# Gate and up of small experts in two matmul passes, with expert weight tiles split in one piece

## The chip, the core and the metric

One core of a Trainium2 chip runs the whole program once. The metric is the device time of that run in microseconds. The profile is one profiled execution of the same program; times inside it count from its first instruction.

## The reference, cut to what matters

A block with a token mixer and a mixture-of-experts layer is followed by a second block with attention, retention and a dense MLP. The change touches the expert layer, and how weight tiles are split in all layers. 512 tokens each go to 8 of 64 experts:

```python
N_EXPERTS, TOP_K, D_MODEL, D_EXPERT = 64, 8, 1024, 256

def swiglu(h, w_gu, w_down):
    gate, up = jnp.split(h @ w_gu, 2, axis=-1)
    return (jax.nn.silu(gate) * up) @ w_down

def expert_block(acc, blk):
    tok, wts, e = blk
    out = swiglu(h_pad[tok], w_gu[e], w_down[e])
    return acc.at[tok].add(out * wts[:, None]), None
```

Gate and up of one expert are a [tokens x 1024] by [1024 x 512] product, down is a [tokens x 256] by [256 x 1024] product. Everything is float32.

## The kernel before, in words

**Split numbers.** Every float32 operand of a large product is held as two tiles of the type float32r: `hi`, a copy that ScalarE (ACT) rounds, and `lo`, the rest, which VectorE (DVE) forms as the difference. `mm3` (lines 142 to 148) makes one product of three matmuls: x_hi by w_hi, x_hi by w_lo, x_lo by w_hi. In the expert layer the tokens are the stationary operand and the weights stream past as 512 columns.

**Weight units.** Weights come in units of 1 MB, 128 partitions of 2048 numbers. `load_unit` (line 113) issues one DMA on SyncE's queue (SP) into one of the `raw` buffers: three, and two more in the expert layer. `split_unit` (line 121) takes a unit in two halves of 1024 columns (`PIECES = 2`): each half has its own pair of tiles `whi`, `wlo`, its ACT copy (line 132) and its DVE difference (line 133). There are six such half tiles (two more in the expert layer, from `grow`, line 1130), given out in turn by `Turns`, and `Rows` (line 55) makes two halves look like one unit. A `raw` buffer is free when both differences are done, a half tile when TensorE (PE) is done with it.

**The expert layer.** `order` sorts the experts by their number of tokens, and `plan` (line 1149) gives each place in that order a capacity (`CAPS`): three of 192, six of 128, 21 of 96, 24 of 64 and 8 of 32, and ahead of them two experts of 128 whose place is fixed. It makes 44 groups: 12 pairs of 64 and 64 tokens, which share a block of 128 rows; 8 pairs of 96 and 32, also one block; 13 single experts of 96; 8 of 128; 3 of 192, in two blocks of 128 and 64. The groups are mixed evenly over the layer. That is 47 blocks, and three units of weights (two for gate and up, one for down) for each of 64 experts. An expert with more tokens than its capacity would be taken up by a loop behind a condition (lines 1312 to 1326).

For each group the rows of its blocks are gathered by an indirect DMA from GpSimd (POOL), turned on PE by `expert_rows` (line 985) into tiles `xT` hi and lo of 8 x 128 columns, and multiplied in `expert_in` (line 998): 8 steps of `mm3` an expert and block, into one PSUM tile `mm` of 512 columns. There the whole block is stationary, also in a pair: each expert of a pair computes all of the block's rows and only its own are read. ACT then takes the silu of the first 256 columns and DVE multiplies by the others (lines 1011 and 1012). `expert_turn` and `expert_out` (lines 1014 and 1025) do the down product of the group before, `expert_parts` and `expert_add` add 384 of the 1024 columns by matmuls into PSUM, and `expert_send` adds the other 640 in DRAM by an indirect DMA. All PSUM tiles of the layer but the sums are four banks of the tag `mm`.

The order on each engine is set by the tile framework's scheduler when the program is built; each engine then works strictly in that order.

Of the kernel before, what the change touches and what calls it, by code (L numbers as in the profile page):

```python
# [10 lines left out]
F = mybir.dt.float32  # L11
R = mybir.dt.float32r
# [9 lines left out]
T = 512  # L22
# [6 lines left out]
UNIT = 2048  # L29
PIECES = 2  # L30
PIECE = UNIT // PIECES
# [23 lines left out]
class Rows:  # L55


    def __init__(self, tiles, n, a):
        self.tiles, self.n, self.rows = tiles, n, a

    def __getitem__(self, at):
        p, k, *rest = at
        return self.tiles[k // self.n][(p, k % self.n, *rest)]


class Kernel:
    def __init__(self, ctx, tc, ins, out):
        self.tc, self.nc, self.ins, self.out = tc, tc.nc, ins, out
        self.ctx = ctx
        pool = lambda name, bufs=1, **k: ctx.enter_context(tc.tile_pool(name=name, bufs=bufs, **k))  # L70
        self.const = pool("const")
        self.raws = Turns((pool("wraw", RAW_BUFS, side="right"), RAW_BUFS))
        self.splits = Turns((pool("wsplit", SPLIT_BUFS * PIECES), SPLIT_BUFS * PIECES))
# [47 lines left out]
    def split_unit(self, parts, a, b, engine=None, rv=None):  # L121

        nc = self.nc
        if rv is None:
            rv = self.load_unit(parts if isinstance(parts, list) else [(None, parts)], a, b)
        n = min(a, a * PIECE // UNIT) if a * b == UNIT else a
        tiles = []
        for k in range(0, a, n):
            sp = self.splits.next()
            hi = sp.tile([128, PIECE], R, tag="hi", name="whi")[:, :n * b].rearrange("p (a b) -> p a b", a=n)  # L130
            lo = sp.tile([128, PIECE], R, tag="lo", name="wlo")[:, :n * b].rearrange("p (a b) -> p a b", a=n)
            nc.scalar.activation(hi, rv[:, k:k + n], AF.Copy)  # L132
            (engine or nc.vector).tensor_sub(lo, rv[:, k:k + n], hi.bitcast(F))  # L133
            tiles.append((hi, lo))
        hv, lv = (Rows([t[i] for t in tiles], n, a) for i in range(2))
# [4 lines left out]
        return hv, lv  # L140
# [21 lines left out]
    def fm_chunk(self, ps, w, x, j, n=T, x0=0):  # L162

        kk = w[0].rows
# [820 lines left out]
    def expert_rows(self, tiles, pp, xg, m=128):  # L985
# [3 lines left out]
        xT = [pool.tile([128, KD, 128], R, tag=tag, name="xT", bufs=2)[:, :, 0:m] for tag in tags]  # L989
        for u in range(2):  # L990
# [4 lines left out]
            self.split_ps(xT[0][:, 4 * u:4 * u + 4], xT[1][:, 4 * u:4 * u + 4], p2)  # L995
        return xT

    def expert_in(self, pp, gu, blocks, between=None):
# [3 lines left out]
        for u in range(2):  # L1002
            w = self.split_unit(gu[u].rearrange("p (k n) -> p k n", k=4), 4, 512)
            for ps, (xT, *_) in zip(pss, blocks):
                for k in range(4):
                    kk = 4 * u + k
                    self.mm3(ps[0:xT[0].shape[2]], [z[:, kk] for z in xT], [z[:, k] for z in w], kk == 0, kk == KD - 1)
            if u == 0 and between:
                between()
        for ps, (xT, a, p0, p1) in zip(pss, blocks):  # L1010
            nc.scalar.activation(a[p0:p1], ps[p0:p1, 0:256], AF.Silu)
            nc.vector.tensor_mul(a[p0:p1], a[p0:p1], ps[p0:p1, 256:512])  # L1012
# [30 lines left out]
    def expert_parts(self, mp, y, row, bufs=2):  # L1043
# [3 lines left out]
        yh, yl = (mp.tile([128, CA], R, tag=f"eys{i}", name="eys", bufs=bufs)[0:m] for i in range(2))  # L1047
        nc.scalar.activation(yh, y[0:m, :CA], AF.Copy)  # L1048
        last = nc.gpsimd.tensor_sub(yl, y[0:m, :CA], yh.bitcast(F))  # L1049
        oh = mp.tile([128, T], R, tag="eoh", name="eoh", bufs=bufs)[0:m]  # L1050
# [36 lines left out]
    def first_block(self):  # L1087
# [9 lines left out]
        with tc.tile_pool(name="route", bufs=1) as keep:  # L1097
# [7 lines left out]
            with ExitStack() as mctx, ExitStack() as ectx:  # L1105
# [24 lines left out]
                def grow():  # L1130
                    hctx.close()
                    sp = ectx.enter_context(tc.tile_pool(name="wsplit2", bufs=PIECES))
                    self.splits = Turns(*splits.pools, (sp, PIECES))
# [12 lines left out]
            self.raws, self.splits = raws, splits  # L1146
# [23 lines left out]
    def experts(self, mp, pp, h2d, cb, acc, shared, gT, sums, grow, ahead, extra):  # L1170
# [42 lines left out]
        def turn(g):  # L1213

            if g < len(groups):
                xT[g] = []
                for b in groups[g][1]:
                    free.append(xg_of[count[1]])
                    xT[g].append(self.expert_rows(tiles, pp, free[-1], b[-1][2]))
# [26 lines left out]
        tiles = more, ("xT0", "xT1")  # L1246
# [9 lines left out]
        for g in range(len(groups) + 1):  # L1256
# [36 lines left out]
            if g < len(groups):  # L1293
# [3 lines left out]
                for j, e in enumerate(es):  # L1297
                    e = number(e)
                    now[2].append(e)
                    self.expert_in(pp, gu(e), [(xT[g][b], a[b], p0, p1) for b, parts in enumerate(bs)  # L1300
                                               for i, p0, p1, _ in parts if i == j], None if j else advance)
# [9 lines left out]
        total = self.further(xp)  # L1311
        with tc.If(total > 0):
            cnt = xp.tile([128, 1], F, name="xcnt")
            nc.vector.memset(cnt, 0.0)
            with tc.For_i(0, total):
# [5 lines left out]
                self.expert_in(pp, gu(ev), [(self.expert_rows(tiles, pp, xgs[0]), a, 0, 128)])  # L1321
                y = mp.tile([128, D], F, tag="ey", name="ey", bufs=2)
                self.expert_out(pp, dn(ev), [(self.expert_turn(more, pp, a), wt, y, 0, 128)])
                self.expert_add(acc, *self.expert_parts(xp, y, row, 1)[0])
# [47 lines left out]
    def each_unit(self, ctx, w, loaded=(), engines=()):  # L1372

        sp = ctx.enter_context(self.tc.tile_pool(name="wsplit3", bufs=PIECES))
# [4 lines left out]
        turns = Turns((base, n - PIECES), (sp, PIECES), (base, PIECES))  # L1379
# [580 lines left out]
```

## Time and profile before

| | us |
|---|---|
| median of 3 runs (lowest, highest) | 2128.33 (2125.3, 2130.84) |
| the profiled execution's own time | 2128.15 |
| its span, first to last instruction | 2126.4 |
| PE busy | 2038.1 (96%) |
| DVE busy | 1425.5 (67%) |
| ACT busy | 1090.8 (51%) |
| POOL busy | 486.2 (23%) |

The span is shorter than the execution's time by 1.75 us. Shares of a whole span are means over stages with different limits, so the table only says that PE is nearly always at work; what a saved instruction is worth has to be read in its stage. In the rows below PE is TensorE's matmuls, PEld its loads of the stationary operand, SPq the queue of SyncE; "DMA share" is the mean busy share of the 16 DMA engines and PEclk the granted share of TensorE's 2.4 GHz.

### The profile page before, as it was taken

The numbers are of one execution on the slowest core, as the hardware profiler recorded it, in microseconds if no ns is written. First come the engines' busy times: TensorE is split into PE (matmuls) and PEld (weight loads), VectorE is DVE, ScalarE is ACT, GpSimd is POOL, SyncE is SP. The second block draws the span as 40 slices with busy tenths as digits, with TensorE's granted clock in tenths as the row PEclk, the third lists the DMA queues.
The fourth block names the chain that finished last, engine by engine and source line by source line (L and its number), as shares of the span: only waits on it lengthen the run. The fifth ranks groups of instructions, "written<-read, shape, count | busy, mean of one in ns | idle before, by whom it ended". The sixth has DMA issues, their size and how long they took to land. (4 is left out here: it accounts for less than half of the span.)

```text
span 2126.4 us, 28083 instructions
## 1 busy us (share of the span) xinstructions
PE 2038.1 (96%) x10311; PEld 1663.4 (78%) x10311; DVE 1425.5 (67%) x2444; ACT 1090.8 (51%) x1569; POOL 486.2 (23%) x307
## 2 busy tenths in 40 slices
PE   7999999999899999999999996999999999999998
PEld 4777888877787788877887784877788878888886
DVE  6667767647899799989999785455853345333344
ACT  7445443233387788878887884334232224232232
POOL 0322231011144343524334213011100001010110
PEclk9999999999899999999999998999999999999999
DMA  7211136633499899999999885312122333222221
GB/s 297 70 41 48 53 111 261 235 110 147 177 322 335 290 341 352 339 325 307 337 336 337 289 290 188 132 60 70 50 89 79 114 115 116 92 100 99 99 80 40
DMA packets 69713, 386.68 MB, mean 182 GB/s; under 512 B 11374, under 2 KB 12351, under 8 KB 30020
## 3 DMA queue, kind: packets, MB, share of 16 engines
q1 hardware_dynamic: 56932, 357.56, 45.6%
q0 software_dynamic: 12640, 27.29, 5.5%
q8 instruction: 82, 1.34, 0.2%
q14 instruction: 59, 0.48, 0.1%
HBM read 369.99 MB, written 23.55 MB: 185 GB/s over the span
## 5 line engine op out<-in xcount | busy, mean ns | idle before, releaser
L133 DVE TENSOR_TENSOR wlo<-raw,whi 128x1024 fp32r<-128x1024 f32 x586 | 728.0, 1258 | 252.0 <-ACT whi L132 244.0
L132 ACT ACTIVATE whi<-raw 128x1024 fp32r<-128x1024 f32 x592 | 621.0, 1057 | 385.6 <-PE mm L147 190.7
L146 PE MATMUL mm<-whi,xT 128*128 128x512 f32 (+2 forms) x536 | 219.7, 410 | 0.1
L147 PE MATMUL mm<-wlo,xT 128*128 128x512 f32 (+2 forms) x536 | 211.9, 395 | 0.0
L148 PE MATMUL mm<-whi,xT 128*128 128x512 f32 (+2 forms) x536 | 211.9, 395 | 0.0
L1039 POOL DMA_INDIRECT cb<-ey,sgi x67 | 130.9, 1954 | 233.4 <-ACT ey L1035 148.4
L146 PE MATMUL mm<-hT,whi 128*128 128x512 f32 x320 | 127.0, 397 | 0.0
L147 PE MATMUL mm<-hT,whi 128*128 128x512 f32 x320 | 125.8, 394 | 0.0
L148 PE MATMUL mm<-hT,wlo 128*128 128x512 f32 x320 | 125.5, 392 | 0.0
L147 PE MATMUL mm<-x,whi 128*128 128x512 f32 x304 | 122.5, 403 | 0.0
L148 PE MATMUL mm<-x,wlo 128*128 128x512 f32 x304 | 120.8, 398 | 0.0
L146 PE MATMUL mm<-x,whi 128*128 128x512 f32 x304 | 120.8, 397 | 0.0
L148 PEld LDWEIGHTS mm<-whi,xT 128*128 128x128 f32 (+2 forms) x536 | 96.8, 181 | 27.8
L146 PEld LDWEIGHTS mm<-whi,xT 128*128 128x128 f32 (+2 forms) x536 | 97.2, 181 | 23.1 <-DVE act L1012 0.5
L1565 POOL TENSOR_TENSOR relu<-relu 128x512 f32<-128x512 f32 x32 | 42.9, 1341 | 315.0 <-ACT relu L1563 315.0
L147 PEld LDWEIGHTS mm<-wlo,xT 128*128 128x128 f32 (+2 forms) x536 | 97.2, 181 | 22.3
L1049 POOL TENSOR_TENSOR eys<-ey,eys 128x384 fp32r<-128x384 f32 (+2 forms) x47 | 79.2, 1686 | 141.2 <-ACT eys L1048 114.3
L148 PE MATMUL mm<-whi,eaT 128*128 128x512 f32 (+2 forms) x268 | 105.8, 396 | 0.4 <-DVE eaT L153 0.2
L147 PE MATMUL mm<-wlo,eaT 128*128 128x512 f32 (+2 forms) x268 | 105.8, 395 | 0.0
L146 PE MATMUL mm<-whi,eaT 128*128 128x512 f32 (+2 forms) x268 | 105.8, 395 | 0.0
L146 PE MATMUL mm<-y,whi 128*128 128x512 f32 (+2 forms) x272 | 103.2, 380 | 0.0
L148 PE MATMUL mm<-y,wlo 128*128 128x512 f32 (+2 forms) x272 | 103.1, 379 | 0.0
(534 smaller groups left out, 4488.9 us busy)
## 6 DMA issues: line engine op xcount, KB each, us to landing
raw<-in_w_expert_gu SPq DMA_DIRECT2D x128, 1024.0 KB
raw<-in_w_expert_down SPq DMA_DIRECT2D x64, 1024.0 KB
raw<-in_w_in SPq DMA_DIRECT2D x41, 1024.0 KB
raw<-in_w_ff SPq DMA_DIRECT2D x32, 1024.0 KB
raw<-in_w_ada SPq DMA_DIRECT2D x24, 1024.0 KB
raw<-in_w_out SPq DMA_DIRECT2D x8, 1024.0 KB
raw<-in_w_v SPq DMA_DIRECT2D x4, 1024.0 KB
raw<-in_w_ret_up SPq DMA_DIRECT2D x4, 1024.0 KB
```

What stands on the lines that cost most here:

```text
L132: nc.scalar.activation(hi, rv[:, k:k + n], AF.Copy)
L133: (engine or nc.vector).tensor_sub(lo, rv[:, k:k + n], hi.bitcast(F))
L146: mm(ps, ah, bh, start=start, stop=False)
L147: mm(ps, ah, bl, start=False, stop=False)
L148: mm(ps, al, bh, start=False, stop=stop)
L1039: self.nc.gpsimd.indirect_dma_start(out=cb, out_offset=bass.IndirectOffsetOnAxis(ap=gi, axis=0), in_=y[p0:p1, CA:], in_offset=None, bounds ...
L1049: last = nc.gpsimd.tensor_sub(yl, y[0:m, :CA], yh.bitcast(F))
L1565: nc.gpsimd.tensor_mul(sq, r, r)
```

## The change

Four things, the first two of which the title names.

- `expert_in`: where a block's part holds up to 64 tokens (the pairs of 64, the 32 of a pair, the second block of a 192), hi and lo of those tokens stand side by side as one stationary operand of up to 128 columns. Two matmuls a step, by w_hi and by w_lo, give x_hi's product in the first rows of the PSUM tile and x_lo's in the rows behind; ACT copies the second lot to a tile `esum`, DVE adds the first, and silu and product follow from `esum`. The product x_lo by w_lo comes along. `expert_rows` lays the tiles out for it; the block of a 96 and a 32 takes four split instructions more.
- `split_unit`: one pair of tiles for the whole unit. In the expert layer (`cuts` is 1 there) one ACT copy and one DVE difference of 2048 columns do it; elsewhere it is still two and two, but the tile is free only as a whole. There are three whole tiles, and one more in the expert layer.
- The last sum (`add()`) stands ahead of the conditional loop instead of behind it.
- The conditional loop shares buffers with the layer.

```diff
 def split_unit(self, parts, a, b, engine=None, rv=None):
-        n = min(a, a * PIECE // UNIT) if a * b == UNIT else a
-        tiles = []
+        n = a // self.cuts if a * b == UNIT else a
+        sp = self.splits.next()
+        hi, lo = (sp.tile([128, UNIT], R, tag=t, name="w" + t)[:, :a * b].rearrange("p (a b) -> p a b", a=a)
+                  for t in ("hi", "lo"))
         for k in range(0, a, n):
-            sp = self.splits.next()
-            hi = sp.tile([128, PIECE], R, tag="hi", name="whi")[:, :n * b].rearrange("p (a b) -> p a b", a=n)
-            lo = sp.tile([128, PIECE], R, tag="lo", name="wlo")[:, :n * b].rearrange("p (a b) -> p a b", a=n)
-            nc.scalar.activation(hi, rv[:, k:k + n], AF.Copy)
-            (engine or nc.vector).tensor_sub(lo, rv[:, k:k + n], hi.bitcast(F))
+            nc.scalar.activation(hi[:, k:k + n], rv[:, k:k + n], AF.Copy)
+            (engine or nc.vector).tensor_sub(lo[:, k:k + n], rv[:, k:k + n], hi[:, k:k + n].bitcast(F))
...
 def expert_rows(self, tiles, pp, xg, parts=((0, 128),)):
+            x = pool.tile([128, KD, 256], R, tag=tags[0], name="xT", bufs=2)
+            if len(parts) == 1:
+                at = 128 if w > 64 else w
+                hi, lo = x[:, :, 0:w], x[:, :, at:at + w]
+                cut, out = [(lambda z: z, hi, lo)], [(hi, lo) if w > 64 else (x[:, :, 0:2 * w],)]
+            elif w == 64:
+                v = x.rearrange("p k (j h w) -> p k h j w", j=2, h=2)
+                cut = [(lambda z: z.rearrange("p k (j w) -> p k j w", j=2), v[:, :, 0], v[:, :, 1])]
+                out = [(x[:, :, 0:128],), (x[:, :, 128:256],)]
+            else:
+                cut = [(lambda z: z[:, :, 0:w], x[:, :, 0:w], x[:, :, 256 - w:256]),
+                       (lambda z: z[:, :, w:m], x[:, :, w:m], x[:, :, m:256 - w])]
+                out = [(x[:, :, 0:w], x[:, :, 256 - w:256]), (x[:, :, w:256 - w],)]
...
 def expert_in(self, mp, pp, gu, blocks, between=None):
-                    self.mm3(ps[0:xT[0].shape[2]], [z[:, kk] for z in xT], [z[:, k] for z in w], kk == 0, kk == KD - 1)
+                    if len(xT) == 2:
+                        self.mm3(ps[0:xT[0].shape[2]], [z[:, kk] for z in xT], [z[:, k] for z in w],
+                                 kk == 0, kk == KD - 1)
+                    else:
+                        for i, z in enumerate(w):
+                            nc.tensor.matmul(ps[0:xT[0].shape[2]], xT[0][:, kk], z[:, k],
+                                             start=kk == i == 0, stop=kk == KD - 1 and i == 1)
...
+                n = p1 - p0
+                s = mp.tile([128, 512], F, tag="esum", name="esum", bufs=2)[p0:p1]
+                nc.scalar.activation(s, ps[n:2 * n], AF.Copy)
+                nc.vector.tensor_add(s, ps[0:n], s)
+                nc.scalar.activation(a[p0:p1], s[:, 0:256], AF.Silu)
+                nc.vector.tensor_mul(a[p0:p1], a[p0:p1], s[:, 256:512])
...
+        add()
         with tc.If(total > 0):
...
-        add()
```

Counted over the whole built program, PE has 280 fewer matmuls of 512 columns (35 parts of up to 64 tokens, 8 each). ACT has 392 copies of 1024 columns fewer and 196 of 2048 more, DVE likewise; each has 35 instructions more for `esum`.

On PE, the end of gate and up of a pair of 64 and 64 tokens, its second unit and the start of the down product behind it; before (the numbers tell buffers apart):

```order
L146 MATMUL mm_6478<-whi_6515,xT_6243 128x512
L147 MATMUL mm_6478<-wlo_6516,xT_6243 128x512
L148 MATMUL mm_6478<-whi_6515,xT_6244 128x512
L146 MATMUL mm_6478<-whi_6515,xT_6243 128x512
L147 MATMUL mm_6478<-wlo_6516,xT_6243 128x512
L148 MATMUL mm_6478<-whi_6515,xT_6244 128x512
L146 MATMUL mm_6543<-whi_6535,eaT_6504 96x512
```

and in the changed program:

```order
L1018 MATMUL mm_6286<-whi_6311,xT_6066 128x512
L1018 MATMUL mm_6286<-wlo_6312,xT_6066 128x512
L1018 MATMUL mm_6286<-whi_6311,xT_6066 128x512
L1018 MATMUL mm_6286<-wlo_6312,xT_6066 128x512
L1041 MATMUL tp_6301<-ident_66,act_6084 128x96 x2
L131 MATMUL mm_6334<-whi_6330,eaT_6304 96x512
```

Each step has two matmuls instead of three, with one stationary tile instead of two, and a unit is one tile.

On DVE, at the same place of the layer; before, the product that frees the PSUM tile stands behind a difference of 1024 columns:

```order
L133 TENSOR_TENSOR wlo_6611<-raw_6608,whi_6610 128x1024
L153 TENSOR_TENSOR eaT_6505<-tp_6501,eaT_6504 128x2x96
L133 TENSOR_TENSOR wlo_6615<-raw_6608,whi_6614 128x1024
L133 TENSOR_TENSOR wlo_6667<-raw_6664,whi_6666 128x1024
L1012 TENSOR_TENSOR act_6468<-act_6468,mm_6478 64x256
L133 TENSOR_TENSOR wlo_6671<-raw_6664,whi_6670 128x1024
```

and in the changed program the addition of 512 columns that frees it comes behind one of 2048:

```order
L120 TENSOR_TENSOR wlo_6394<-raw_6391,whi_6393 128x2048
L138 TENSOR_TENSOR eaT_6305<-tp_6301,eaT_6304 128x2x96
L1031 TENSOR_TENSOR esum_6323<-mm_6286,esum_6323 64x512
L120 TENSOR_TENSOR wlo_6448<-raw_6445,whi_6447 128x2048
L1033 TENSOR_TENSOR act_6276<-act_6276,esum_6323 64x256
```

Of the 35 additions of the program, 10 stand directly behind two whole differences.

On ACT, again there, in the changed program:

```order
L137 ACTIVATE eaT_6304<-tp_6301 128x2x96
L1030 ACTIVATE esum_6323<-mm_6286 64x512
L1032 ACTIVATE act_6276<-esum_6323 64x256
L1056 ACTIVATE ey_6308<-mm_6334,swt_5194 96x512
L1069 ACTIVATE eys_6358<-ey_6308 96x384
```

Before, one silu stood there in place of the first two `esum` rows. The silu now waits for DVE's addition, and the copy `ey` that frees the next PSUM tile stands behind it; in 3 of the 35 cases the two follow each other directly like this, in the others at least one more instruction lies between.

## Rows read from the trace of the kernel before

**Rows 1.** Windows by stage: busy us of each engine (x instructions), PEclk, DMA share, GB/s.

```profile
600.00:1290.00 690.00, 685.20 (x3493) 545.95 (x3492) 613.24 (x889) 567.55 (x755) 270.54 (x153) 1.00 0.92 321
610.00:1290.00 680.00, 675.48 (x3430) 538.70 (x3429) 604.18 (x862) 559.35 (x744) 266.13 (x150) 1.00 0.92 322
...
1290.00:2126.40 836.40, 802.57 (x3681) 655.63 (x3679) 392.27 (x680) 268.43 (x412) 92.61 (x66) 0.98 0.27 93
```

**Rows 2.** Timeline of the expert layer, ten matmul starts apart: start us, us, engine, line.

```profile
816.02 0.39 PE L146 MATMUL mm<-whi,xT 128*128 128x512 f32 x1
...
818.35 0.40 PE L147 MATMUL mm<-wlo,eaT 128*128 128x512 f32 x1
```

**Rows 3.** Waits of PE, ACT and DVE, 610:1290: us in total, times, longest.

```profile
PE tp L908 <- DVE oh L903: 1.2, 3, 0.8
...
ACT whi L132 <- PE mm L148: 69.8, 134, 5.5
...
DVE wlo L133 <- ACT whi L132: 52.7, 81, 3.6
```

**Rows 4.** Waits of SyncE's DMA queue, 600:1290.

```profile
SPq L118 <- DVE wlo L133: 447.9, 156, 8.8
```

**Rows 5.** Groups by line and form, 610:1290: busy us, mean ns of one, idle before.

```profile
L133 DVE TENSOR_TENSOR wlo<-raw,whi 128x1024 fp32r<-128x1024 f32 x373 | 459.6, 1253 | 56.9 <-ACT whi L132 52.7
L132 ACT ACTIVATE whi<-raw 128x1024 fp32r<-128x1024 f32 x370 | 388.9, 1057 | 72.8 <-PE mm L148 69.8 <-DVE wlo L133 0.7 <-DVE srow L915 0.3
...
L153 DVE TENSOR_TENSOR xT<-tp,xT 128x512 fp32r<-128x512 f32 x56 | 35.9, 680 | 3.2 <-ACT xT L152 2.9
L152 ACT ACTIVATE xT<-tp 128x512 fp32r<-128x512 f32 x56 | 30.3, 594 | 6.1 <-PE mm L147 4.5 <-PE tp L994 1.2
...
L153 DVE TENSOR_TENSOR xT<-tp,xT 128x384 fp32r<-128x384 f32 x24 | 12.2, 550 | 1.0 <-ACT xT L152 0.7
...
L1012 DVE TENSOR_TENSOR act<-act,mm 64x256 f32<-64x256 f32 x27 | 11.2, 414 | 1.4 <-ACT act L1011 1.1
...
L152 ACT ACTIVATE xT<-tp 128x384 fp32r<-128x384 f32 x24 | 10.4, 487 | 0.2
L1011 ACT ACTIVATE act<-mm 64x256 f32<-64x256 f32 x27 | 10.2, 378 | 8.4 <-PE mm L148 8.4
...
L153 DVE TENSOR_TENSOR eaT<-tp,eaT 128x192 fp32r<-128x192 f32 x13 | 4.6, 351 | 0.9 <-ACT eaT L152 0.9
L152 ACT ACTIVATE eaT<-tp 128x192 fp32r<-128x192 f32 x13 | 4.1, 313 | 0.0
```

**Rows 6.** The tile wlo, 610:1290: DVE's differences, duration ns min/median/max.

```profile
L133 DVE TENSOR_TENSOR wlo<-raw,whi x373: 1204/1218/2776, 609.7 to 1280.8; 128x1024 fp32r<-128x1024 f32 x187
```

**Rows 7.** DMA of 610:1290: packets, and MB and share of 16 engines by queue.

```profile
DMA packets 38001, 218.85 MB, mean 322 GB/s; under 512 B 6867, under 2 KB 6867, under 8 KB 14265
...
q1 hardware_dynamic: 26641, 194.00, 75.6%
q0 software_dynamic: 11304, 24.16, 15.7%
```

**Rows 8.** Windows of 50 us: the densest of DVE and of the DMA engines in the layer.

```profile
600.00:650.00 50.00, 49.72 (x252) 40.12 (x251) 48.30 (x72) 43.56 (x58) 28.08 (x11) 1.00 0.93 343
...
1050.00:1100.00 50.00, 49.83 (x253) 40.15 (x252) 46.04 (x66) 43.61 (x58) 15.52 (x11) 1.00 0.98 363
```

**Rows 9.** Window of 10 us with the highest transfer rate of the layer.

```profile
920.00:930.00 10.00, 9.78 (x72) 8.10 (x71) 8.28 (x25) 6.48 (x9) 3.27 (x2) 1.00 1.00 405
```

**Rows 10.** Timeline at the layer's end: the sums of the last block, on PE.

```profile
1284.10 1.78 PE L1058 MATMUL acc<-eys,eoh 96*128 96x384 f32 x8
```

More of the change, by code (lines that the diff above doesn't have):

```diff
@@ L29 @@
 UNIT = 2048
-PIECES = 2
-PIECE = UNIT // PIECES
 VEC = {}
@@ L52, in next @@
         return order[(self.n - 1) % len(order)]
[L55 to L63, printed above, removed]
 class Kernel:
@@ L72, in __init__ @@
         self.raws = Turns((pool("wraw", RAW_BUFS, side="right"), RAW_BUFS))
-        self.splits = Turns((pool("wsplit", SPLIT_BUFS * PIECES), SPLIT_BUFS * PIECES))
+        self.splits = Turns((pool("wsplit", SPLIT_BUFS), SPLIT_BUFS))
+        self.cuts = 2
         self.dram = pool("scratch", space=DRAM)
@@ L139, in split_unit @@
             self.ticking = False
-        return hv, lv
+        return hi, lo
     def mm3(self, ps, a, b, start, stop):
@@ L162, in fm_chunk @@
     def fm_chunk(self, ps, w, x, j, n=T, x0=0):
-        kk = w[0].rows
+        kk = w[0].shape[1]
         for k in range(kk):
@@ L983, in gather, with expert_rows @@
                                           bounds_check=T - 1, oob_is_err=False)
-    def expert_rows(self, tiles, pp, xg, m=128):
+    def expert_rows(self, tiles, pp, xg, parts=((0, 128),)):
         nc = self.nc
         pool, tags = tiles
-        xT = [pool.tile([128, KD, 128], R, tag=tag, name="xT", bufs=2)[:, :, 0:m] for tag in tags]
+        m = parts[-1][1]
+        w = parts[0][1]
+        if len(tags) == 2:
+            hi, lo = (pool.tile([128, KD, 128], R, tag=tag, name="xT", bufs=2)[:, :, 0:m] for tag in tags)
+            cut, out = [(lambda z: z, hi, lo)], [(hi, lo)]
+        else:
[12 more added lines that the diff above has]
+                out = [(x[:, :, 0:w], x[:, :, 256 - w:256]), (x[:, :, w:256 - w],)]
         for u in range(2):
@@ L994, in expert_rows, with expert_in @@
                 nc.tensor.transpose(p2[:, k], xg[0:m, c:c + 128], self.ident[0:m, 0:m])
-            self.split_ps(xT[0][:, 4 * u:4 * u + 4], xT[1][:, 4 * u:4 * u + 4], p2)
-        return xT
-    def expert_in(self, pp, gu, blocks, between=None):
+            for some, hi, lo in cut:
+                self.split_ps(hi[:, 4 * u:4 * u + 4], lo[:, 4 * u:4 * u + 4], some(p2))
+        return out
+    def expert_in(self, mp, pp, gu, blocks, between=None):
         nc = self.nc
@@ L1218, in turn @@
                     free.append(xg_of[count[1]])
-                    xT[g].append(self.expert_rows(tiles, pp, free[-1], b[-1][2]))
+                    xT[g].append(self.expert_rows(tiles, pp, free[-1], [p[1:3] for p in b]))
                     rows_of.setdefault(g, []).append(count[1])
@@ L1245, in experts @@
         more = grow()
-        tiles = more, ("xT0", "xT1")
+        tiles = more, ("xT",)
         room(mp, AHEAD2)
@@ L1299, in experts @@
                     now[2].append(e)
-                    self.expert_in(pp, gu(e), [(xT[g][b], a[b], p0, p1) for b, parts in enumerate(bs)
-                                               for i, p0, p1, _ in parts if i == j], None if j else advance)
+                    self.expert_in(mp, pp, gu(e), [(xT[g][b][i], a[b], p0, p1) for b, parts in enumerate(bs)
+                                                   for i, (k, p0, p1, _) in enumerate(parts) if k == j],
+                                   None if j else advance)
                     finish()
```

30 lines of the change are left out of this document (16 added, 14 removed).

## The prediction

> **What bounds the kernel now.** I read the windows by stage first, because the change acts almost only in the expert layer, from 600 to 1290 us [rows 1]. In those 690 us TensorE is busy for 685.2, VectorE for 613.2, ScalarE for 567.6, and the 16 DMA engines have a mean share of 0.92. Four resources are close together; the reader is to see that TensorE is first, but with little distance to the next. The timeline says that TensorE's busy time is real: eleven matmuls start evenly between 816.02 and 818.35 [rows 2], 0.233 us apart, at the granted clock of 1.00, that is 2.4 GHz [rows 1]. The waits say the same from the other side [rows 3]: TensorE's longest wait for a tile is 1.2 us in all of 680, while ScalarE's copies wait 69.8 us for TensorE to give a split tile back and VectorE's differences 52.7 us for those copies. SyncE's loads wait 447.9 us for VectorE to free a raw buffer [rows 4]: data come as fast as they are used up. So TensorE sets the pace, and the work behind it runs ahead until its buffers are full.
>
> A rule that speaks against this reading: the Trainium skill, Perfetto Trace Analysis, section "Identifying the Most-Contended Engine", says that matmul busy time misleads and that the busy share of the weight loads is to be taken instead. Here that share is 546.0 of 690, 79% [rows 1]; by the rule TensorE would have a fifth of its time to spare, and matmuls taken away would give nothing: the time would stay at 2128 us. The even starts and the direction of the waits decide against it here, and I keep a small chance for it (the fourth case below).
>
> **The change part by part.** The sum is made against the profiled execution's own 2128.15 us, which is 0.2 below the median of 2128.33.
>
> *Matmuls removed.* 35 parts of up to 64 tokens lose 8 matmuls each: 280 x 0.233 = 65.2 us of TensorE [rows 2]. Fewer weight loads go with them. TensorE's stage would be 690 - 65 = 625 us if nothing else bound it.
>
> *Whole differences and copies.* The trace has no instruction of 2048 columns here. Above, it costs two halves, so nothing is saved; below, I go by how cost grows: VectorE from 680 ns at 512 columns [rows 5] to a median of 1218 at 1024 [rows 6], 538 per 512 columns, so 1218 + 1076 = 2294 ns, 142 less than two halves; ScalarE from 594 to 1057 [rows 5], so 1983 ns, 131 less. I take these, since rows of both engines grow by a fixed amount per column. For the layer's 187 units (373 halves [rows 5]) it is 26.6 us off VectorE and 24.5 off ScalarE.
>
> *Sums added.* 35 copies and 35 additions of 512 columns, the first of them out of PSUM. Nearest rows: 594 ns on ScalarE, 680 on VectorE [rows 5], hence 20.8 and 23.8 us. The silu and the product keep 378 and 414 ns [rows 5]; reading SBUF they could be a little cheaper or dearer, at most some tens of ns each, under 2 us. The 8 blocks of 96 and 32 split in two cuts, twice a block: on VectorE 550 + at most 351 instead of 680 [rows 5], 3.5 us more in all; on ScalarE 487 + 313 instead of 594, 3.3 us. Net, VectorE 613.2 - 26.6 + 23.8 + 3.5 = 613.9 us and ScalarE 567.6 - 24.5 + 20.8 + 3.3 = 567.2: both unchanged. What one part of the change saves on them the other spends.
>
> *Transfers.* None are added or taken away: 0.92 x 690 = 635 us of all 16 engines [rows 1].
>
> *What is late next.* Without TensorE's 65 us the highest floors are the DMA engines' 635, TensorE's 625 and VectorE's 614. None is reached at 100%: the densest 50 us of this layer show the DMA engines at 0.98 and VectorE at 48.3 of 50 [rows 8]. 635 / 0.98 = 648 us, and VectorE's 613.9 / 0.966 = 636. So I put the stage at 648, a gain of 42 of the 65; the wait that takes the place is ScalarE's for a raw tile that has not landed, and TensorE's behind it. The bounds: 690 - 625 = 65 if the DMA share is no floor; 690 - 661 = 29 if the DMA engines stay at 0.96.
>
> *Is the share a floor?* In the same section the skill wants the transfer rate, not the engines' occupancy, as the measure for DMA, and its section "Engine Utilization" gives 358 GB/s as a core's peak, about 435 at most for one core alone. By that, 321 GB/s is 90% or 74%, the floor is 619 us or lower, and the case below in which TensorE stays the bound would hold. The trace shows 405 GB/s over one stretch of 10 us [rows 9], so 358 is no limit here; but at shares of 0.98 the mean of 50 us is 363 GB/s [rows 8], because row gathers and scatters take 15.7% of the engines for 24 of 219 MB [rows 7]. I stay with the share.
>
> *Other stages.* Elsewhere a unit is still split in two cuts, but its tile comes free as a whole. Where that is late once, it costs a half's copy and difference, 1.06 + 1.22 = 2.3 us [rows 5, 6]; at two stage entries (the output projection, the second block) 4.6 us. The scheduler also moves some differences behind other work, which can as well gain. From 1290 us on TensorE is busy 802.6 of 836.4 us [rows 1] and covers the rest. I take 0, with ends of -5 and +5. The sums ahead of the condition are 8 matmuls of 1.78 us [rows 10] that TensorE does at the same place either way: 0, at most 1.8. If no loop pass runs, its buffers cost nothing.
>
> The sum: 2128.15 - 42 = **2086 us**, 2073 to 2099 with the DMA share between 1.00 and 0.96.
>
> **Rivals.** (1) *TensorE stays the bound.* The share of DMA is elastic, loads just overlap more, and VectorE fits. For it: 405 GB/s at 920 us [rows 9], and loads are never waited for now. Against: both next floors lie within 10 to 11 us of TensorE's 625. Time: 2128 - 65 = 2063.
>
> (2) *Every group keeps its own bound.* The four split tiles and five raw buffers may not carry a surplus from one group to the next. The plan has 20 x 72 + 21 x 36 + 3 x 72 = 2412 matmuls, 562 us; the other 128 of 690 are 2.7 us for each of 47 blocks, so a pair took 72 x 0.233 + 2.7 = 19.5 us. Now its VectorE work is 6 x 2.29 + (604.2 - 459.6) / 47 [rows 1, 5] + two sums, 18.6 us or 19.2 at the density above; its transfers are 6 units of 2.78 us (75.6% of 680 by 185 units of 194 MB) and 2.3 of queue 0 (15.7% of 680 by 47) [rows 7], 19.0 or 19.3. A pair gains 0.3 us, 20 pairs 6; the three experts of 192 gain 8 x 0.233 each, 5.6. Against it: nine units of buffers are three experts' weights, and single experts and pairs alternate. Time: 2116.
>
> (3) *The sum holds PSUM.* A bank was free after silu, half a difference and product, 0.38 + 1.22 + 0.41 = 2.0 us; now after copy, addition and what stands ahead of it on VectorE: 0.59 + 2.29 + 0.68 = 3.6 with one whole difference, 5.9 with two, as the built order has it for 10 of 35. There are four banks, and behind the silu, which waits for the addition, ScalarE has the copies that free the others. If TensorE had to wait out all of it, 25 x 1.6 + 10 x 3.9 = 79 us come back for 65 saved: 2128 + 14 = 2142, slower. It decides from 65 / 35 = 1.9 us a sum. Against it: the matmuls behind it go to the three other banks, so only what is left after those are used up is a wait.
>
> (4) *No change.* Something other than TensorE already set the pace, as in the rule above, or waits return all of it: 2128.
>
> That the change does not do what it says is not open: the built order has the 280 matmuls fewer.
>
> **How the numbers follow.** Chances: 0.56 for the forecast, 0.15 for (1), 0.14 for (2), 0.08 for (4), 0.07 for (3). A measurement of this kernel tells 0.3% (6.4 us) from no change. Faster by more are the forecast, (1) and (2), 0.85; the same 0.08; slower 0.07. The range of 8 in 10 takes in the forecast's 2073 to 2099, (1) with 2063 less a little for other stages, and (2) with 2116: 2061 to 2116; the other two stay outside.
>
> **What would show it.** Right: the stage from about 600 us ends near 1248; DMA share about 0.98 in it; matmuls still 0.233 us apart where they run, but TensorE with some 20 us of gaps; differences of about 2.3 us and copies of about 2.0; ScalarE's wait for TensorE nearly gone, waits for landings in its place. Wrong: TensorE without gaps (1); VectorE full while TensorE waits in every pair (2); long waits of matmuls for the copies out of PSUM or the additions (3); or time lost before 600 or after the layer, which I put at nothing.

## The result, and the profile after

The change makes the kernel slower: 2148.86 us median of 4 runs (2141.99 to 2151.66) against 2127.07 (2125.3 to 2130.84, 4 runs); ratio 1.0097, 95% interval 1.0072 to 1.0121. I had forecast 2086 with a range of 2061 to 2116. The profiled execution after took 2151.66 us, the slowest of the four. Its first matmul on gathered rows comes at 585.5 us (585.7 before) and from the layer's end to the second block's first relu it takes 480.1 us (481.4 before); all of the loss lies in the expert layer, whose sums are taken out of PSUM from 1321.8 us on, 24.8 us later than the 1297.0 of before.

The windows of the layer, from 600 us to its end, first of the kernel before and then of the change; the columns are those of [rows 1]:

```profile
600.00:1297.00 697.00, 692.01 (x3522) 551.25 (x3520) 613.24 (x889) 567.57 (x756) 270.64 (x153) 1.00 0.91 318
```

```profile
600.00:1322.00 722.00, 664.81 (x3252) 508.33 (x3250) 619.15 (x757) 558.35 (x625) 328.89 (x153) 0.96 0.89 310
```

Nothing is full any more. TensorE is idle for 57 us where it was idle for 5; its granted clock is 0.96 of full in the mean, some 0.04 x 722 = 29 us of matmul work; and the transfers' share is lower than before, 0.89. So 65 us of matmuls went and some 52 + 29 came back as gaps and as slower matmuls; the 9 us left in the busy time make up the measured 25 more. The 29 is an estimate from a rounded share, and what the 9 are made of is not shown.

Waits of TensorE and of GpSimd, 610 to 1290 us (us in total, times, longest), first in the kernel before, where the scatter `cb` and the difference `eys` have other line numbers, then in the change:

```profile
PE acc L1058 <- POOL eys L1049: 1.1, 2, 0.9
...
POOL cb L1039 <- DMA cb<-ey,sgi: 45.3, 13, 8.1
```

```profile
PE acc L1079 <- POOL eys L1070: 19.5, 9, 3.6
PE mm L131 <- ACT eaT L137: 8.4, 9, 2.2
PE tp L1041 <- DVE act L1033: 4.8, 6, 1.7
PE mm L1018 <- DVE wlo L120: 3.6, 5, 1.0
...
POOL cb L1060 <- DMA cb<-ey,sgi: 62.9, 14, 6.2
POOL eys L1070 <- ACT eys L1069: 60.0, 17, 6.8
```

TensorE's longest waits do not go back to weight units that have not landed, as I had said, but to `eys`, the difference that GpSimd forms ahead of the additions into `acc`. GpSimd's own wait until the scatter before has landed was there before the change too, 45.3 us; TensorE was idle for 5 us all the same. One of TensorE's waits, in the timelines of GpSimd, TensorE and VectorE (start us, us, instruction, idle before it):

```profile
857.84 8.29 POOL L1060 DMA_INDIRECT cb<-ey,sgi  x1 [4.89 <-DMA cb<-ey,sgi]
865.71 1.45 POOL L1070 TENSOR_TENSOR eys<-ey,eys 96x384 fp32r<-96x384 f32 x1
...
863.26 0.40 PE L131 MATMUL mm<-whi,xT 128*128 128x512 f32 x1
867.21 1.48 PE L1079 MATMUL acc<-eys,eoh 96*128 96x384 f32 x7 [3.55 <-POOL eys L1070]
...
869.47 0.63 PE L132 MATMUL mm<-wlo,xT 128*128 128x512 f32 x1
869.90 0.63 PE L133 MATMUL mm<-whi,xT 128*128 128x512 f32 x1
...
856.82 4.48 DVE L120 TENSOR_TENSOR wlo<-raw,whi 128x2048 fp32r<-128x2048 f32 x2
...
862.62 2.28 DVE L120 TENSOR_TENSOR wlo<-raw,whi 128x2048 fp32r<-128x2048 f32 x1
```

The scatter waits 4.89 us until the scatter before it has landed, then its own issue takes 8.29 us while VectorE works through whole differences; `eys` stands behind it, TensorE waits 3.55 us, and its next matmuls start 0.43 us apart in place of 0.23 [rows 2]: it runs at 1.2 GHz.

The groups of the new instructions, 610 to 1290 us (busy us, mean ns | idle before), against [rows 5]:

```profile
L120 DVE TENSOR_TENSOR wlo<-raw,whi 128x2048 fp32r<-128x2048 f32 x183 | 423.1, 2325 | 40.2 <-ACT whi L119 38.8
...
L119 ACT ACTIVATE whi<-raw 128x2048 fp32r<-128x2048 f32 x183 | 347.8, 1912 | 35.7 <-PE mm L1018 20.4 <-PE mm L133 12.5 <-DMA raw<-in_w_expert_down 1.1
...
L1031 DVE TENSOR_TENSOR esum<-mm,esum 64x512 f32<-64x512 f32 x27 | 18.4, 680 | 2.1 <-ACT esum L1030 1.4
...
L1030 ACT ACTIVATE esum<-mm 64x512 f32<-64x512 f32 x27 | 16.0, 594 | 14.0 <-PE mm L1018 13.5
```

All four have the price that I gave them, within 4%. One price that I had kept did rise: the product, which now reads `esum` (414 ns before [rows 5]).

```profile
L1033 DVE TENSOR_TENSOR act<-act,esum 64x256 f32<-64x256 f32 x27 | 13.6, 502 | 3.6 <-ACT act L1032 3.3
```

That is 88 ns for each of 35, 3 us of VectorE. The prices were not the error.

### The profile page after: what moved, and what is told of

Read it like the earlier page. It is cut to its first block, busy times and chain, and to the rows that moved or that the text cites. A ratio compares the mean times of both kernels' runs of the same rounds, so it can differ in the third digit from the quotient of the medians.

```text
span 2150.0 us, 26943 instructions
## 1 busy us (share of the span) xinstructions
PE 2011.1 (94%) x10031; PEld 1620.6 (75%) x10031; DVE 1434.5 (67%) x2302; ACT 1070.3 (50%) x1427; POOL 549.6 (26%) x307
## 5 line engine op out<-in xcount | busy, mean ns | idle before, releaser
L120 DVE TENSOR_TENSOR wlo<-raw,whi 128x1024 fp32r<-128x1024 f32 (+1 forms) x393 | 709.6, 1823 | 247.7 <-ACT whi L119 242.1
L119 ACT ACTIVATE whi<-raw 128x1024 fp32r<-128x1024 f32 (+1 forms) x399 | 577.8, 1468 | 370.7 <-PE mm L132 211.1
L1060 POOL DMA_INDIRECT cb<-ey,sgi x67 | 155.6, 2323 | 258.7 <-ACT ey L1056 134.0
L966 POOL DMA_INDIRECT xg<-h2d,sgi x47 | 101.2, 2152 | 78.4 <-DVE srow L900 33.5
L1018 PE MATMUL mm<-wlo,xT 128*128 128x512 f32 (+1 forms) x280 | 114.2, 408 | 3.6 <-DVE wlo L120 3.6
L1018 PE MATMUL mm<-whi,xT 128*128 128x512 f32 (+1 forms) x280 | 115.6, 413 | 0.1
L131 PE MATMUL mm<-whi,xT 128*96 128x512 f32 (+1 forms) x256 | 109.0, 426 | 3.1 <-ACT ey L1056 2.9
L1056 ACT ACTIVATE ey<-mm,swt 64x512 f32<-64x512 f32 (+3 forms) x134 | 90.0, 680 | 41.9 <-PE mm L133 23.8
L132 PE MATMUL mm<-wlo,xT 128*96 128x512 f32 (+1 forms) x256 | 105.2, 411 | 2.9 <-DVE wlo L120 2.9
L1079 PE MATMUL acc<-eys,eoh 128*128 128x384 f32 (+2 forms) x376 | 85.7, 356 | 22.7 <-POOL eys L1070 21.6
L133 PE MATMUL mm<-whi,xT 128*96 128x512 f32 (+1 forms) x256 | 104.7, 409 | 0.0
```

The lines of the kernel that those rows point to most:

```text
L119: nc.scalar.activation(hi[:, k:k + n], rv[:, k:k + n], AF.Copy)
L120: (engine or nc.vector).tensor_sub(lo[:, k:k + n], rv[:, k:k + n], hi[:, k:k + n].bitcast(F))
L131: mm(ps, ah, bh, start=start, stop=False)
L132: mm(ps, ah, bl, start=False, stop=False)
L133: mm(ps, al, bh, start=False, stop=stop)
L966: self.nc.gpsimd.indirect_dma_start(out=xg[0:gi.shape[0]], out_offset=None, in_=h2d, in_offset=bass.IndirectOffsetOnAxis(ap=gi, axis=0), b ...
```

## The experiments

Each ratio, with its 95% interval, is to runs of the kernel before that were made beside it. Six theories are tried, and the expectations name them by letter: A, a long instruction holds up what is queued behind it; B, the whole tile comes free too late; C, the sums hold up the chain; D, VectorE's fill and the waits in its order set the pace; E, the scatters on GpSimd do, each behind the landing of the one before; G, the transfers do. e5, e7, e8, e12 and e13 leave something out and serve only to tell what a part costs.

| run | median us | ratio |
|---|---|---|
| e1_twopass_half | 2146.66 | 1.0090 (1.0072 to 1.0108) |
| e2_whole_only | 2143.37 | 1.0071 (1.0050 to 1.0091) |
| e3_two_cuts | 2130.95 | 1.0015 (1.0003 to 1.0026) |
| e4_eys_dve | 2134.31 | 1.0031 (1.0019 to 1.0044) |
| e5_drop_lo | 2104.27 | 0.9879 (0.9854 to 0.9904) |
| e6_sums_only | 2142.97 | 1.0076 (1.0059 to 1.0093) |
| e7_two_cb | 2124.40 | 0.9983 (0.9972 to 0.9994) |
| e8_no_down_lo | 2101.11 | 0.9877 (0.9859 to 0.9896) |
| e9_two_cuts_two_cb | 2127.70 | 0.9996 (0.9985 to 1.0006) |
| e10_before_two_cb | 2134.91 | 1.0029 (1.0017 to 1.0040) |
| e11_half_two_cb | 2123.97 | 0.9981 (0.9971 to 0.9992) |
| e12_drop_two_cb | 2106.17 | 0.9883 (0.9860 to 0.9906) |
| e13_no_down_load | 2094.75 | 0.9851 (0.9837 to 0.9866) |
| e14_early_merge | 2133.55 | 1.0029 (1.0019 to 1.0039) |
| e15_half_early_merge | 2129.05 | 1.0010 (1.0000 to 1.0020) |
| e16_whole_tile_two_cuts | 2128.67 | 1.0008 (0.9998 to 1.0019) |
| e17_half_merged | 2124.40 | 0.9985 (0.9976 to 0.9993) |
| e18_two_cuts_merged | 2127.36 | 1.0004 (0.9995 to 1.0013) |

The scheduler gives each version an order of its own, so part of any difference can be the order; no run here holds the order fixed. e9 and e11, which differ in tiles alone, are 4 us apart, e17 and e18 3, but e1 and e3 16. No run takes out the earlier last sum, the shared buffers of the loop or the four split instructions more of the blocks of 96 and 32 by themselves.

### The two parts apart

e1 takes `split_unit` back to half tiles. e2 is the kernel before with the new `split_unit`. e3 and e4 are the change with one line each:

```diff
 def grow():                                   # e3
-                    self.cuts = 1
 def expert_parts(self, mp, y, row):           # e4
-        last = nc.gpsimd.tensor_sub(yl, y[0:m, :CA], yh.bitcast(F))
+        last = nc.vector.tensor_sub(yl, y[0:m, :CA], yh.bitcast(F))
```

> The changed kernel with the weight tiles of before: half tiles of 1024 columns, two copies and two differences a unit; gate and up of small parts in two passes. Theory A (the long instruction: a difference of 2.3 us holds up what stands behind it on VectorE, and GpSimd's eys beside it, until TensorE waits): the loss goes, the gain of fewer matmuls shows, 2075 to 2105. Theory B (the tile that comes free only as a whole): the same here, 2075 to 2105. Theory C (the sums of the two passes hold up the chain): still about 2149, no lower than 2130. In the profile A and B have the additions into acc waiting for eys by some 4 us in all as before (47 us with the change), C still by tens of us.

> The kernel before with only the second part of the change: one tile pair a unit, one copy and one difference of 2048 columns in the expert layer, three passes as before. Theories A and B: slower than before by at least what the whole change lost, 2150 to 2185, with TensorE waiting for eys. Theory C: 2128 within 6 us, since VectorE and ScalarE only get shorter.

> The changed kernel, whole tiles, but two copies and two differences a unit in the expert layer too. Tells the long instruction from the whole tile. Theory A: 2075 to 2110, eys at about the 1.66 us of before and the differences at 1.2. Theory B: 2140 to 2155, as with the change. Theory C: 2140 to 2155 too, and then e1 is no faster either.

> The changed kernel with the difference of eys on VectorE in place of GpSimd (47 differences of 384 columns more on VectorE, some 0.55 us each, 26 us; the waits of the additions into acc for GpSimd, 47 us in the layer, cannot occur). Theory A in its narrow form (only GpSimd's eys is late): 2148 less most of 47, 2105 to 2125. Theory A in its wide form (everything in order behind a long difference is late, eys only the most seen): the wait moves to eys on VectorE, 2135 to 2160. Theories B and C: 2140 to 2165.

Each part alone loses: the two passes 18 us on half tiles (e1) and 3 on whole tiles with two cuts (e3), the whole split 15 (e2). In the change the whole split costs 18 us against e3, but only 2 against e1, which has the weight tiles of before. The pattern fits none of the three theories alone: C is right that two passes do not pay as the kernel stands, A that the long instruction costs. e4 ends just under the range of A's wide form, 15 us below the change. The 47 us of waits for `eys` in the expectations of e1 and e4 count the same waits twice, 21.6 us at the matmuls and 25.4 at their weight loads; so A's narrow form was worth some 22 us, not 47. `eys` is the most seen wait, but not all. In e1 TensorE's waits read

```profile
PE acc L1094 <- POOL eys L1085: 26.7, 11, 8.0
PE mm L146 <- DVE esum L1046: 5.1, 1, 5.1
```

### What each part is worth by itself

e5 leaves out the product x_lo by w_hi of small parts. e6 adds the sums to the kernel before, and with them only the loop's shared buffers. e7 is the change with its scatters by turns into two DRAM tensors; e8 is e3 without the differences of the down units. The excerpts show each edit's main line.

```diff
 def expert_in(...)                            # e5, parts up to 64
-                    self.mm3(ps, [z[:, kk] for z in xT], [z[:, k] for z in w], ...)
+                        for i, z in enumerate(w):
+                            nc.tensor.matmul(ps, xT[0][:, kk], z[:, k], ...)
 def expert_in(...)                            # e6, parts up to 64
+                nc.scalar.activation(s, ps[p0:p1], AF.Copy, scale=0.0)
+                nc.vector.tensor_add(s, ps[p0:p1], s)
 def finish(): ...                             # e7
-                        self.expert_send(y_, gi, p0, p1, cb)
+                        self.expert_send(y_, gi, p0, p1, (cb, self.cb2)[sent[0] % 2])
 def expert_out(...)                           # e8, on e3
-        w = self.split_unit(dn..., 2, D)
+        w = self.split_unit(dn..., 2, D, low=False)
```

> The kernel before with the third matmul of a step (x_lo by w_hi) left out for parts of up to 64 tokens: 280 matmuls of 512 columns fewer, as in the change, and nothing else; no sums, no other tiles (the output lacks that small product). What are 65 us of TensorE worth alone? Theory C (the sums eat the gain): 2063 to 2090. Theory D (behind TensorE the work of VectorE, ScalarE and the waits in their order fill the stage almost to the same length): 2105 to 2130, with TensorE's idle time grown by what was taken away. Theory E (the scatters into DRAM, each behind the landing of the one before, set the pace on GpSimd): as D, with GpSimd's waits for landings of cb grown.

> The kernel before, all three matmuls a step, with the copy to esum and the addition for parts of up to 64 tokens (the copy is scaled by zero, so that the sum is unchanged): the cost of the sums alone, 21 us of ScalarE and 24 of VectorE, while TensorE has its 65 us. Theory C: the sums hold up the chain, 2140 to 2165. Theory D: TensorE still covers most of VectorE's work, but VectorE rises to 0.93 of the stage, 2128 to 2145.

> The changed kernel with scatters going by turns into two DRAM tensors, so that one does not wait for the landing of the one right before it (the second tensor is not added up: half of the far columns' sums is missing). Theory E: GpSimd's waits for landings (63 us with the change) and with them the late eys go, 2105 to 2130. Theories C and D: 2140 to 2152, eys is late for other reasons.

> The run with two passes, whole tiles and two cuts (e3_two_cuts), with the differences of the down units left out: their wlo is not formed and whi takes its place in the matmuls (the output lacks that product). TensorE's work is as in e3, VectorE has 64 x 2 x 1.25 = 160 us less. Theory D (VectorE's fill sets the stage): the gain of the fewer matmuls appears, 2060 to 2090. Theory E (GpSimd): stays within 10 us of e3's 2131. Theory C, whose sums are still there: 2105 to 2131.

The 280 matmuls alone give 24 us of their 65, just under D's range and far from C's; e5's four runs spread from 2095.06 to 2111.62, so the 24 are known to some 5 us. The sums alone cost 15, inside both ranges, and TensorE's longest sum of waits in e6 is the turn's for `act`:

```profile
PE tp L1027 <- DVE act L1019: 5.2, 8, 1.2
```

Together that would be 9 gained, and e1 lost 18 (e3 3): the two add up worse than singly. Scatters by turns win 24 us back from the change, as E said, and TensorE's wait for `eys` falls from 19.5 to 6.6 us:

```profile
PE acc L1079 <- POOL eys L1070: 6.6, 6, 2.3
```

But with VectorE relieved of 140 us (632.2 us busy in e3's layer, 492.6 in e8's) e8 gains 30 against e3, though scatters still wait for landings; it lies between D's range and C's. So D and E both hold a part. Its layer has the highest mean share of transfers of any run, 0.94:

```profile
600.00:1270.40 670.40, 640.67 (x3256) 490.76 (x3254) 492.60 (x818) 575.28 (x811) 236.00 (x153) 1.00 0.94 334
```

How far VectorE also slows GpSimd shows in the groups of e3 and then of e8 (600 to 1320 us), which have the same scatters and the same 47 differences of `eys`:

```profile
L1060 POOL DMA_INDIRECT cb<-ey,sgi x67 | 158.8, 2370 | 244.5 <-ACT ey L1056 127.6 <-DMA cb<-ey,sgi 78.9 <-DVE wlo L120 10.5
L1070 POOL TENSOR_TENSOR eys<-ey,eys 128x384 fp32r<-128x384 f32 (+2 forms) x47 | 92.0, 1959 | 93.6 <-ACT eys L1069 75.9 <-issue 13.4 <-PE mm L133 4.0
```

```profile
L1061 POOL DMA_INDIRECT cb<-ey,sgi x67 | 120.0, 1791 | 257.9 <-ACT ey L1057 125.0 <-DMA cb<-ey,sgi 64.6 <-ACT whi L119 30.5
L1071 POOL TENSOR_TENSOR eys<-ey,eys 128x384 fp32r<-128x384 f32 (+2 forms) x47 | 59.8, 1273 | 137.0 <-ACT eys L1070 126.2 <-issue 10.5
```

### Scatters by turns, with the sum made whole

e9 to e12 are e3, before, e1 and e5 with the edit of e7, and the second tensor added to the first when the second block begins:

```diff
             nc.sync.dma_start(fs[0][:, CA:], cb[rows[0], :])
+            nc.gpsimd.dma_start(fs[0][:, CA:], self.cb2[rows[0], :], accum_op=OP.add)
```

> e3_two_cuts (two passes, whole tiles, two cuts) with scatters by turns into two DRAM tensors, both added up at the start of the second block by an adding DMA (some 1 to 4 us more there). Theory E (scatters, each behind the landing of the one before, bound the layer once TensorE is quicker): 2098 to 2112, about the 24 us below e3 that the change gained in e7. Theory D (what is left is VectorE's fill, 0.92 of the stage in e3): 2120 to 2131, the freed wait returns elsewhere. With the sums at +15 and the matmuls at -24 as measured alone, nothing below 2095 is expected of any theory.

> Control: the kernel before with the two DRAM tensors. Its TensorE is busy for 99.5% of the stage, so nobody waits for scatters on the path: 2126 to 2133 (the adding DMA costs some 1 to 4 us) by all theories. A gain of over 6 us would say that scatters already held up the kernel before.

> e1_twopass_half (two passes with half tiles, 2146.7) with the two DRAM tensors. Theory E: 2105 to 2128, and eys is waited for by under 10 us in place of 27. Theory D: 2135 to 2148. Between them: the part of e1's loss that scatters explain.

> e5_drop_lo (280 matmuls fewer and nothing else, 2104.3) with the two DRAM tensors. If the scatters are what kept 41 of the 65 us back: 2063 to 2085 (Theory E). If VectorE and ScalarE or the transfers' share keep it back (Theory D): 2095 to 2106.

The adding costs 8 us behind the layer, more than I had put down, and puts e10 2 us above its range: from the layer's end to the first relu of the second block e10 takes 490.0 us where before takes 481.4 (e11 490.8 where e1 takes 480.1). With 8 us taken off, scatters by turns are worth some 31 us on e1, 11 on e3, 6 on e5, and nothing on the kernel before, where TensorE covers them; the 6 lie within the spread of e5's runs. So on half tiles the loss of the two passes hangs on the scatters' landings: e1's 18 us lost become some 11 gained. The 16 us between e1 and e3 hang on them too, since e11 and e9 are 4 apart the other way. e11 falls into E's range, though TensorE's waits for `eys` are 13.7 us there (610 to 1290 us) and not under 10. e9 falls into D's range and e12 0.2 us above the end of D's: with 280 matmuls fewer, no sums and no scatter behind another (e12), the layer is still only 29 us shorter (1268.3 for 1297.0).

### What keeps the rest

e13 is e12 with the down units' loads left out, so that the output has the wrong down weights. e16 is e2 with the instructions cut in two.

```diff
 def expert_out(...)                           # e13, on e12
-        w = self.split_unit(dn..., 2, D)
+        w = self.split_unit(None, 2, D, None, self.kept...)
 def grow():                                   # e16, on e2
-                    self.cuts = 1
```

> e12_drop_two_cb (280 matmuls fewer, no sums, scatters by turns: 2106, its layer 29 us shorter) with the loads of the down units left out: one tile loaded once is split for every expert (the output lacks the right down weights), and one raw buffer fewer rotates for gate and up. Copies, differences and matmuls stay, 64 of 192 MB of loads go. Theory G (transfers: in e8 and e12 both, the layer ends at about 685 us after its start with a DMA share of 0.94, and that share is what a mean over the layer can reach): 2060 to 2085. Theory D (VectorE at 0.91 of the layer and the waits in its order): within 8 us of 2106.

> The kernel before with whole tiles, but two copies and two differences a unit in the expert layer too (e2_whole_only, 2143.4, with the long instructions cut). Theory A (the long instruction keeps what stands behind it on ScalarE and VectorE from TensorE): 2125 to 2132, as before. Theory B (the tile that comes free as a whole): 2138 to 2148, as e2.

The windows of the layer in e12, then in e13:

```profile
600.00:1268.00 668.00, 641.66 (x3241) 502.49 (x3239) 600.66 (x889) 546.93 (x755) 285.98 (x153) 0.99 0.93 332
```

```profile
600.00:1250.00 650.00, 629.44 (x3236) 501.37 (x3234) 593.91 (x887) 551.51 (x756) 381.86 (x153) 0.99 0.73 240
```

With a third of the loads gone the share falls to 0.73; the layer is 18.7 us shorter in these two profiles (the slowest of e12's four runs and the fastest of e13's), the medians are 11 apart. Transfers did hold something back, but the time lies between G's range and D's, and TensorE is still idle for 21 us. e16 settles the whole split: the same tiles as e2, and with two instructions a unit the 15 us are gone but for 2. It is the long instruction (A), not the tile (B), with the order that the scheduler then gives. The windows of the layer in e2, then in e16:

```profile
600.00:1314.70 714.70, 701.13 (x3540) 556.23 (x3538) 596.67 (x709) 540.00 (x573) 295.96 (x154) 1.00 0.89 313
```

```profile
600.00:1299.80 699.80, 694.98 (x3541) 555.49 (x3539) 613.91 (x897) 554.62 (x761) 253.38 (x153) 1.00 0.92 321
```

TensorE is idle for 13.6 us in e2 and for 4.8 in e16, so 9 of the 15 us are idle time; the rest is not broken down here. In e2 TensorE has no long wait, but short ones for work of VectorE and GpSimd:

```profile
PE mm L131 <- DVE eaT L138: 3.2, 2, 1.6
PE acc L1043 <- POOL eys L1034: 2.1, 3, 0.8
PE mm L131 <- DVE xT L138: 1.5, 1, 1.5
PE tp L893 <- DVE xT L138: 1.3, 1, 1.3
```

### Versions that might beat both

e14 and e15 (on e3 and e1) add the second tensor to the first in DRAM ahead of the last five scatters; e17 and e18 (on e1 and e3) load it into idle tiles and add it on VectorE and GpSimd.

```diff
+                        if sent[0] == n:                               # e14, e15
+                            nc.gpsimd.dma_start(cb, self.cb2, accum_op=OP.add, max_dma_last_dim=640)
+                    e = nc.gpsimd if t else nc.vector                  # e17, e18
+                    e.tensor_add(fs[t][:, CA:], fs[t][:, CA:], f2[t])
```

> e9_two_cuts_two_cb with the second DRAM tensor added to the first in DRAM ahead of the last five scatters in place of adding DMAs after the layer, which cost about 8 us between the layer's end and the second block. All theories: 8 us less than 2127.7, 2115 to 2122, faster than the kernel before; above 2126 the merge waits at the layer's end.

> The same on half tiles (e11_half_two_cb, 2124.0): 2112 to 2119 by all theories. It is the two-pass part of the change alone, with scatters that don't wait for the one right before them.

> e11_half_two_cb (two passes on half tiles, scatters by turns into two DRAM tensors, 2124.0) with the second tensor loaded into tiles that stand idle at that point and added by VectorE and GpSimd before the first block's sums are taken, in place of adding DMAs, which put about 8 us between the layer's end and the second block. 1 to 2 us remain: 2115 to 2121, faster than the kernel before by 0.3 to 0.6%. 2124 or above says that the adding DMAs were not what cost the 8 us.

> The same with whole tiles and two cuts (e9_two_cuts_two_cb, 2127.7): 2118 to 2125. All theories of the layer expect the same of it as of the half tiles; a difference of over 6 us between the two would be the order that the scheduler gives, not the tile.

All four miss. In e14 the next scatter waits 23.7 us for the DRAM addition, and `eys` behind it keeps TensorE waiting for up to 12.7 us. In e17 the layer's end and the first relu are 489.7 us apart, so the adding DMAs were not what cost the 8 us. The profiles show where they go: at the second block's start TensorE waits for the squares of the norm (`tp` for `csq`) 18.0 us in the kernel before, 28.0 in e10 and 27.8 in e17. The norm needs both tensors, by whichever way they are added. Still, e11 and e17, the two passes on half tiles with scatters by turns, are 0.15 to 0.2% faster than the kernel before and 1.1 to 1.2% faster than the change; they leave nothing out. Their intervals just exclude no difference from the kernel before, and the gain is under the 0.3% that I had taken as telling. e5, e8, e12 and e13 are faster but leave something out.

## Why the prediction was wrong

*What bounds the kernel.* Right: e5 takes matmuls away and gains 24 us. The rule that I weighed against it (the Trainium skill, Perfetto Trace Analysis, "Identifying the Most-Contended Engine": weight loads, not matmul time), as I read it, would have given e5 nothing; e5's 24 us disagree with it here.

*Matmuls removed.* The size was right, the worth was not. Of 65 us, 24 arrive; e12 and e13 show where more may lie: by the medians 6 us once scatters do not wait for one another, which is within the runs' spread, and 11 once loads are fewer.

*Whole differences and copies: the first step that failed.* I counted them as 26.6 and 24.5 us saved. The durations came out as priced (2325 and 1912 ns), but an engine that works in strict order also has to finish such an instruction before it turns to what TensorE waits for. That cost 15 us in e2, and in the change 18 against e3 but 2 against e1; where scatters go by turns it is some 5 to 8 (e7 against e9 and e11, with 8 us taken off these for the adding). I had weighed busy time and never the wait that a longer instruction puts ahead of `eaT`, `act` and `ey`.

*Sums added: the second.* Again the price was right (594 and 680 ns) and "both unchanged" was right for busy time: VectorE 619.2 us and ScalarE 558.4 in the whole layer, 613.9 and 567.2 forecast. But the sums stand in the chain from matmul to `act` to the turn. Alone they cost 15 us (e6), where TensorE's longest sum of waits, 5.2 us, is the turn's for `act`; the rest is not broken down here.

*What is late next, and the stage at 648: the step that carried the number.* 635 / 0.98 took the share of the densest 50 us [rows 8] for one that a whole layer can hold. The highest mean of any run here is 0.94 (e8). The layer is not as long as its highest floor; while TensorE was full, it hid the waits of VectorE, ScalarE, GpSimd and the scatters, and each showed once it was not. I had named none of GpSimd's. With scatters by turns the change gets back 24 us (e7) and e1 31, while the kernel before gains nothing from it (e10). The slower clock after gaps, 29 us in the change, stood in no term either, since the layer before ran at 1.00 throughout [rows 1].

*Is the share a floor?* The Trainium skill's rule in the same section, the rate in place of the share, would have left TensorE as the bound. e13, where fewer loads at an unchanged TensorE shorten the layer, speaks for the share, but only in part: 11 us for a third of the loads.

*Other stages* were 0, as said. *Rivals:* the third had the sign, with 0.07, but not the place: matmuls waited for a sum once in e1 (5.1 us), and not among the longest waits of the change. The second had the right idea, a bound for each group, with the wrong resource: it counted VectorE and transfers and left out the two scatters of a pair, some 8 us each from issue to landing in the change, one after the other. Its VectorE time for a pair, 18.6 us, comes to 18.2 from the terms it names, and 19.5 less the 19.3 of transfers is 0.2 us a pair, not 0.3; its time would have been 2118 in place of 2116.

What stays open: how the 65 us divide exactly among VectorE's order, landings and transfers, since the reliefs do not add up; and how much of each part's loss is only the scheduler's order.

## What to carry to other kernels

When the one full engine of a stage is relieved, don't put the stage at the next highest floor: list every chain that this engine now hides (the in-order queues, GpSimd's, transfers that wait for a landing) and price the waits that begin. Merging two instructions into one saves busy time but lengthens the wait of all that is queued behind, so on an engine that others wait for it can cost more than it saves. Test such parts one at a time first: here each lost by itself.

## What the runs showed of the hardware that I had not expected

TensorE's granted clock fell to 1.2 GHz after gaps of TensorE, though not after each (a gap of 2.22 us at 1242.5 us in the change left it at 1.00). Windows of the change around the wait shown above, with no matmul in the second:

```profile
852.00:864.00 12.00, 11.49 (x55) 8.49 (x53) 11.17 (x12) 10.29 (x11) 7.11 (x2) 1.00 1.03 394
864.00:867.00 3.00, 0.00 (x0) 0.00 (x0) 2.83 (x5) 2.95 (x5) 3.00 (x2) 1.00 0.99 385
868.00:875.00 7.00, 7.00 (x28) 5.68 (x27) 4.87 (x5) 2.38 (x3) 2.45 (x2) 0.76 0.92 306
```

So a gap can cost more than its length: here 3.5 us idle, then eight matmuls from 869.05 us on that start 0.43 us apart in place of 0.23, by estimate 1.6 us more.

GpSimd's instructions got longer as VectorE did more: `eys` takes 1273 ns in e8 and 1959 in e3, and a scatter's issue 1791 and 2370 (spans on GpSimd are rough). Single issues are as long as 8.29 us in the change, but 7.20 in the kernel before already. For `eys` the trace shows what lengthens it. Of the 31 of 128 x 384 in the change, the ten during which VectorE forms no `wlo` take 1.00 to 1.52 us; the longest takes 5.75, and 4.18 us of two `wlo` fall into it:

```profile
804.34 5.75 POOL L1070 TENSOR_TENSOR eys<-ey,eys 128x384 fp32r<-128x384 f32 x1
...
803.97 2.28 DVE L120 TENSOR_TENSOR wlo<-raw,whi 128x2048 fp32r<-128x2048 f32 x1
...
806.97 2.27 DVE L120 TENSOR_TENSOR wlo<-raw,whi 128x2048 fp32r<-128x2048 f32 x1
...
810.15 2.01 PE L1079 MATMUL acc<-eys,eoh 128*128 128x384 f32 x7 [3.24 <-POOL eys L1070]
```

GpSimd was late here already, by a scatter that had waited 6.23 us for a landing; but the 4.7 us that `eys` takes beyond 1.0 are more than TensorE's whole wait of 3.24. So a difference on VectorE can stand on TensorE's path by way of GpSimd. The Trainium skill, SBUF — State Buffer, "Who interferes with whom", says that a VectorE instruction with two inputs in SBUF contends with a GpSimd instruction that reads SBUF, which agrees for `eys`. It says that it does not contend with one that only writes; which side the scatters' issue belongs to, no run here shows: some that lie wholly under a difference take 1.4 us, others are several times as long.
